# Which engine makes the low halves of the first expert product's panels: a one-argument change in a Trainium2 kernel

## The chip, the cores and the metric

The kernel runs on one core of one Trainium2 chip. A core has five engines with queues of their own: TensorE (PE: matmuls, and PEld: weight loads beside them), VectorE (DVE), ScalarE (ACT), GpSimd (POOL) and SyncE (SP, which here only issues DMAs). Each engine works its own queue in order; engines meet through semaphores. The metric is the device time of one execution, in microseconds (us).

## The reference, cut to what matters

The model is a chain of two blocks over 512 tokens of width 1024: a gated delta rule layer and a sliding-window attention layer, then a layer that mixes an mLSTM with forgetting attention, and at its end a product-key retrieval over 16384 experts of one neuron each. Only this last part is touched by the change:

```python
def block(xb):                       # 128 tokens
    scores = einsum('thpc,hpnc->thpn', (xb @ w_query)..., keys32)
    val, idx = lax.top_k(scores, 16)              # per head and half
    top_s, pos = lax.top_k(cand, 16)              # of 16 x 16 sums
    ids = ...                                     # 8 heads x 16 experts per token
    gate = softmax(top_s)
    act = gelu(einsum('ted,td->te', u_emb[ids], xb))
    return einsum('te,ted->td', gate * act, v_emb[ids])
```

The kernel computes three of the four blocks of 128 tokens densely: gelu of all 16384 first products, times a dense gate matrix G that is zero outside the chosen experts, times all of `v`. For the fourth block (tokens 0 to 127) it gathers the chosen rows of `u` and `v`.

## The kernel before, in words

All large products are made in split float32: an operand is written as a high half (rounded to the fast matmul type by ACT, line 233) and a low half (the operand minus its high half, line 235), and three matmuls (lines 315 to 317, `mm3`) make the product. `halves` does this for a panel of 128 x 1024: the cast is always on ACT, and the subtraction is on DVE, or on POOL if the caller passes `lo_on_pool=True`. Panels of the earlier stages come from `Feed`, which passes it; so does `route1`, with the 16 panels of the query weights.

`stage_p` is the last stage, from about 1517 us of the profile on. Its parts are these.

- `route1` (line 1495 on): the queries, their scores and the first choice of 16, all tokens.
- The stretch ahead of the loop, about 1637 to 2009 us. `route2` makes the second choice of 16 for each of the four token blocks on DVE (`top16`, line 1534 and after, rows by line 1561 and after). `build_g` builds the dense gates G for three token blocks in 32 steps each: two one-hot tiles `o0` (DVE, line 1598) and `o1` (in one of four steps POOL, line 1601, four instructions; else DVE, line 1603), `o0` times the gate (in two of four steps POOL, line 1605; else ACT, line 1608), four small matmuls into `pG` (line 1611), an ACT copy, and every eight steps a DMA of the result to DRAM. Woven between these are 48 (`SPILL`) jobs of class `First`. In this stretch a planner orders the instructions of each engine's queue when the kernel is built.
- The loop, about 2009 us to the end. Its order is written out by hand (`manual_schedule`): 208 jobs, 80 `First` and 128 `Second`, of which the first six are `First`, the last ten `Second`, and between them about five `First` to eight `Second`. At step n the code issues the loads of job n, the preparations of job n-1 and the matmuls of job n-2 (`LEAD = 2`), and after the preparation the late uses of gathered rows (DVE, `LATE = 2` gathers behind their issue) and the issue of new gathers (POOL, line 1470).

A `First` loads one panel of `u` transposed (`raw`, 512 KB, line 1348), makes its halves `whi` (ACT) and `wlo` (line 1351 calls `halves`), multiplies in 24 matmuls of 384 columns into `pj`, and applies gelu on ACT into `hg` (line 1357). A `Second` loads a panel of `v` (line 1412), multiplies `hg` by the gates on DVE (`W`, line 1417), splits `W` (ACT `Wh`, line 212, and DVE `Wl`, line 213), makes the panel's halves `whio` (ACT) and `wloo` (DVE, line 235), and multiplies in 18 matmuls of 512 columns into six accumulators `acc`.

The 256 gathers (128 of rows of `u`, then 128 of `v`) are indirect DMAs issued by POOL; each is used by one DVE instruction: line 1474 (row product with `xt`, summed) or line 1479 (scaled and added to `x`). Panels of `u`, panels of `v` and gathered rows share one ring of eight `raw` buffers; the tiles `whi` and `wlo` have two buffers each.

The lines that the change and the steps below speak of: 221 to 236 (`halves`), 1351 (`First.prep`), 1353 to 1361 (`First.work`), 1414 to 1420 (`Second.prep`), the loop with `ld.load()`, `pr.prep()` and `wk.work()`, and `gather`.

Of the kernel before, what the change touches and what calls it, by code (L numbers as in the profile page):

```python
# [1327 lines left out]
def stage_p(k, out):  # L1328
# [3 lines left out]
    with pool(tc, name="sp1", bufs=1) as s1:  # L1332
# [7 lines left out]
        class First:  # L1340
# [7 lines left out]
                nc.sync.dma_start(self.raw, a["uT"][self.i])  # L1348

            def prep(self):  # L1350
                self.pan = k.halves(self.raw, lo_on_pool=True, bufs=2)

            def work(self):
                p = k.acc()
# [300 lines left out]
```

## Time and profile before

| what | us |
|---|---|
| median of three runs | 2926.01 |
| lowest and highest of them | 2915.71, 2930.39 |
| the profiled execution | 2929.05 |
| its span, first to last instruction | 2927.3 |

The page gives the busy time of each engine over the span, its course in 40 slices of 73 us, and groups of instructions. Further views of the trace are the busy time in chosen stretches, the waits of a stretch grouped by who waited for whom, the instructions grouped by line and shape, and the instructions in order of time. In a group of instructions "idle before" is the idle time of the engine just before them, and the arrow names what ended it. A DVE instruction's duration runs some 0.07 us into that of the next one, so busy times of a stretch, which count an instant once, are a little below the sum of durations.

### The profile page before, as it was taken

The page shows a single profiled execution, that of the slowest core. Times are in us where ns is not written, and L with a number is a line of the kernel's source. Part 1 is how long each engine was busy: PE and PEld are TensorE (multiplying, and loading weights), DVE is VectorE, ACT ScalarE, POOL GpSimd, SP SyncE. Part 2 cuts the span into 40 slices and gives each one's busy share as a digit, 9 for nine tenths or more (in the row PEclk, how much of TensorE's full clock was granted, in tenths as well). Part 3 has the DMA queues.
Part 4 walks back from the last instruction along what each step waited for, and adds up shares of the span by engine and source line. Part 5 has one row for each costly group of instructions (what it writes and reads, how often), then busy time and mean ns, then how long its engine had stood idle before and what let it go on. Part 6 is the DMA issues. An engine that isn't in the chain of part 4 may idle for free.

```text
span 2927.3 us, 39434 instructions
## 1 busy us (share of the span) xinstructions
PE 2759.3 (94%) x14291; PEld 2266.0 (77%) x14291; DVE 2048.9 (70%) x4211; ACT 1126.7 (38%) x2300; POOL 1112.6 (38%) x737
## 2 busy tenths in 40 slices
PE   7999999989999999899989888899999999999998
PEld 5777777767676777677668788799888888888887
DVE  6666666675565556445657999955888888888887
ACT  5444444344434334233322254554333333333332
POOL 0100000000101133331113488797666665666652
PEclk9999999999999999998799998899999999999999
DMA  4111111122122122210022333456889899888886
GB/s 145 51 58 58 58 58 58 44 79 66 58 66 65 58 66 63 72 58 30 15 94 80 106 137 132 174 184 249 307 314 322 294 319 320 299 309 306 310 307 233
DMA packets 170463, 440.92 MB, mean 151 GB/s; under 512 B 13932, under 2 KB 79756, under 8 KB 168604
## 3 DMA queue, kind: packets, MB, share of 16 engines
q1 hardware_dynamic: 133404, 304.17, 30.9%
q0 software_dynamic: 36864, 134.23, 12.5%
q8 instruction: 113, 1.85, 0.3%
q14 instruction: 82, 0.67, 0.1%
HBM read 401.60 MB, written 36.75 MB: 150 GB/s over the span
## 4 chain that ended last, share of the span: by engine, by line
PE 47%; DVE 21%; issue 13%; DMA 7%; ACT 6%; POOL 5%; ACTq 0%; SPq 0%; POOLq 0%; DVEq 0%
PE pj L315 8%; PE pj L316 8%; PE pj L317 8%; DVE x L1479 5%; DVE raw L1474 4%; ACT whio L233 3%; POOL wlo L235 2%; DMA raw<-in_uT_dram 2%; PE pG L1611 2%; DMA raw<-in_u_dram,ids 2%; DVE W L1417 2%; DVE wloo L235 1%; POOL o L1601 1%; PE po L922 1%; PE fo L1305 1%
## 5 line engine op out<-in xcount | busy, mean ns | idle before, releaser
L315 PE MATMUL pj<-hThi,whi 128*128 128x384 f32 (+2 forms) x1664 | 606.3, 365 | 4.6 <-ACT hg L1357 3.9
L317 PE MATMUL pj<-hThi,wlo 128*128 128x384 f32 (+2 forms) x1664 | 598.0, 359 | 5.0 <-POOL wlo L235 4.8
L316 PE MATMUL pj<-hTlo,whi 128*128 128x384 f32 (+2 forms) x1664 | 600.2, 361 | 0.0
L235 POOL TENSOR_TENSOR wlo<-raw,whi 128x1024 fp32r<-128x1024 f32 x144 | 368.5, 2559 | 366.8 <-ACT whi L233 339.1
L315 PEld LDWEIGHTS pj<-hThi,whi 128*128 128x128 f32 x1664 | 319.9, 192 | 32.9 <-ACT hg L1357 4.2
L317 PEld LDWEIGHTS pj<-hThi,wlo 128*128 128x128 f32 x1664 | 319.0, 192 | 31.1 <-POOL wlo L235 10.5
L316 PEld LDWEIGHTS pj<-hTlo,whi 128*128 128x128 f32 x1664 | 319.7, 192 | 24.4 <-DVE hTlo L213 0.7
L316 PE MATMUL acc<-wloo,Wh 128*128 128x512 f32 x768 | 307.8, 401 | 22.8 <-DVE wloo L235 21.0
L315 PE MATMUL acc<-whio,Wh 128*128 128x512 f32 x768 | 301.5, 393 | 0.6 <-ACT whio L233 0.4
L317 PE MATMUL acc<-whio,Wl 128*128 128x512 f32 x768 | 300.3, 391 | 0.0
L212 ACT CAST Wh<-W 128x384 fp32r<-128x384 f32 x128 | 65.7, 514 | 479.2 <-DVE W L1417 469.4
L1474 DVE SCALAR_TENSOR_TENSOR raw<-raw,xt 128x1024 f32<-128x1024 f32 x128 | 225.6, 1795 | 34.1 <-DMA raw<-in_u_dram,ids 25.6
L1479 DVE SCALAR_TENSOR_TENSOR x<-raw,act,x 128x1024 f32<-128x1024 f32 x128 | 237.7, 1857 | 3.8 <-DMA raw<-in_v_dram,ids 1.6
L233 ACT CAST whi<-raw 128x1024 fp32r<-128x1024 f32 x144 | 150.3, 1044 | 144.6 <-issue 106.5
L316 PEld LDWEIGHTS acc<-wloo,Wh 128*128 128x128 f32 x768 | 144.1, 188 | 78.5 <-DVE wloo L235 51.4
L1470 POOL DMA_INDIRECT raw<-in_u_dram,ids x128 | 186.8, 1459 | 37.1 <-issue 24.5
L235 POOL TENSOR_TENSOR wlo<-wraw,whi 128x1024 fp32r<-128x1024 f32 x52 | 124.2, 2402 | 188.0 <-ACT whi L233 187.9
L235 DVE TENSOR_TENSOR wloo<-raw,whio 128x1024 fp32r<-128x1024 f32 x128 | 156.8, 1225 | 49.8 <-ACT whio L233 49.8
L1470 POOL DMA_INDIRECT raw<-in_v_dram,ids x128 | 170.2, 1329 | 49.5 <-issue 26.3
L315 PEld LDWEIGHTS acc<-whio,Wh 128*128 128x128 f32 x768 | 144.1, 188 | 32.0 <-ACT whio L233 4.0
L317 PEld LDWEIGHTS acc<-whio,Wl 128*128 128x128 f32 x768 | 144.2, 188 | 28.4
L682 POOL TENSOR_TENSOR kbe<-qk,beg 128x512 f32<-128x512 f32 x8 | 8.4, 1051 | 378.4 <-DVE qk L575 378.4
(417 smaller groups left out, 5620.6 us busy)
## 6 DMA issues: line engine op xcount, KB each, us to landing
raw<-in_uT_dram SPq DMA_DIRECT2D x128, 512.0 KB, 4.1
raw<-in_v_dram SPq DMA_DIRECT2D x128, 512.0 KB, 6.7
wraw<-in_wa_dram SPq DMA_DIRECT2D x48, 512.0 KB, 3.6
G<-stage SPq DMA_DIRECT2D x12, 2048.0 KB, 7.2
Gt<-G SPq DMA_DIRECT2D x32, 768.0 KB, 8.4
wraw<-in_wb_dram SPq DMA_DIRECT2D x32, 512.0 KB, 3.8
wraw<-in_wmt_dram SPq DMA_DIRECT2D x20, 512.0 KB, 3.5
H<-hg SPq DMA_DIRECT2D x48, 192.0 KB, 2.5
```

What stands on the lines that cost most here:

```text
L212: self.nc.scalar.copy(hi, src)
L233: nc.scalar.copy(hi, raw)
L235: eng.tensor_tensor(out=lo, in0=raw, in1=hi.bitcast(F32), op=ALU.subtract)
L315: nc.tensor.matmul(out, wh, mh, start=first, stop=False)
L316: nc.tensor.matmul(out, wh, ml, start=False, stop=False)
L317: nc.tensor.matmul(out, wl, mh, start=False, stop=last)
L922: nc.tensor.matmul(po[:, (4 * b + h) * 64 : (4 * b + h + 1) * 64], PT[:, h * nst + st, :], V[:, s0 // P + st, g * 64 : (g + 1) * 64], star ...
L1417: nc.vector.tensor_tensor(out=split_t(w), in0=split_t(hold.pop(self.i)), in1=gates[self.i // 4][:, :, self.i % 4, :], op=ALU.mult)
L1470: nc.gpsimd.indirect_dma_start(out=g, out_offset=None, in_=src, in_offset=bass.IndirectOffsetOnAxis(ap=ids[:, j : j + 1], axis=0))
L1474: nc.vector.scalar_tensor_tensor(g, g, 1.0, xt0, op0=ALU.mult, op1=ALU.mult, accum_out=act[:, j : j + 1])
L1479: nc.vector.scalar_tensor_tensor(k.x[:, 0, :], g, act[:, j : j + 1], k.x[:, 0, :], op0=ALU.mult, op1=ALU.add)
L1611: nc.tensor.matmul(p[:, n * P : (n + 1) * P], o1[:, n, :], o0[:, n, :], start=True, stop=True)
```

## The change

`First.prep` no longer passes `lo_on_pool=True`, so that the subtraction of line 235 is issued on DVE for the 128 panels of the first product: 48 ahead of the loop and 80 in it. POOL keeps the one-hot tiles and gate products of `build_g`, the panels of `route1` and of the earlier stages, and the issue of the gathers. Buffers, loads and the order of the loop's code stay.

```diff
             def prep(self):
-                self.pan = k.halves(self.raw, lo_on_pool=True, bufs=2)
+                self.pan = k.halves(self.raw, bufs=2)
```

## Rows read from the trace of the kernel before

**Rows 1.** The page: busy us of each engine (share of the span), instructions
```profile
PE 2759.3 (94%) x14291; PEld 2266.0 (77%) x14291; DVE 2048.9 (70%) x4211; ACT 1126.7 (38%) x2300; POOL 1112.6 (38%) x737
```

**Rows 2.** Busy time by stretch: stretch, its us, engines, PE clock, DMA share, GB/s
```profile
1640.00:1900.00 260.00, 213.32 (x1241) 204.42 (x1240) 255.66 (x515) 127.21 (x266) 193.55 (x125) 0.90 0.42 145
1900.00:2009.00 109.00, 104.10 (x667) 103.12 (x667) 60.25 (x58) 59.32 (x132) 97.82 (x69) 0.96 0.45 161
2009.00:2923.00 914.00, 888.33 (x4231) 762.97 (x4229) 752.58 (x773) 303.16 (x418) 557.62 (x333) 1.00 0.87 306
```

**Rows 3.** Waits of the loop, 2009 to 2923 us: total us, times, longest
```profile
POOL wlo L235 <- ACT whi L233: 205.8, 67, 5.9
...
DVE Wl L213 <- ACT Wh L212: 85.3, 128, 1.4
PEld acc L316 <- DVE wloo L235: 51.4, 78, 1.1
...
DVE wloo L235 <- ACT whio L233: 49.8, 128, 1.0
```

**Rows 4.** Instructions by line and shape, loop: count | busy us, mean ns | idle before
```profile
L1479 DVE SCALAR_TENSOR_TENSOR x<-raw,act,x 128x1024 f32<-128x1024 f32 x128 | 237.7, 1857 | 3.8 <-DMA raw<-in_v_dram,ids 1.6
L1474 DVE SCALAR_TENSOR_TENSOR raw<-raw,xt 128x1024 f32<-128x1024 f32 x127 | 224.3, 1800 | 25.8 <-DMA raw<-in_u_dram,ids 25.6
L235 DVE TENSOR_TENSOR wloo<-raw,whio 128x1024 fp32r<-128x1024 f32 x128 | 156.8, 1225 | 49.8 <-ACT whio L233 49.8
...
L235 POOL TENSOR_TENSOR wlo<-raw,whi 128x1024 fp32r<-128x1024 f32 x79 | 202.9, 2568 | 233.2 <-ACT whi L233 205.8 <-PE acc L317 27.4
```

**Rows 5.** Single lines, whole span: duration ns min/median/max, first and last start
```profile
L1474 DVE SCALAR_TENSOR_TENSOR raw<-raw,xt x128: 1212/1220/3546, 1965.5 to 2451.7; 128x1024 f32<-128x1024 f32 x128
L1479 DVE SCALAR_TENSOR_TENSOR x<-raw,act,x x128: 1276/1285/3427, 2453.6 to 2918.1; 128x1024 f32<-128x1024 f32 x128
L1598 DVE TENSOR_TENSOR o<-cst,selT x96: 664/692/2887, 1688.0 to 1998.9; 128x512 f32<-128x512 f32 x96
...
L1534 DVE TENSOR_TENSOR cand<-val x32: 398/418/2617, 1643.8 to 1856.2; 128x256 f32<-128x256 f32 x32
```

**Rows 6.** In order of time, loop: start us, duration us, engine, line, instruction
```profile
2203.47 1.04 ACT L233 CAST whi<-raw 128x1024 fp32r<-128x1024 f32 x1
...
2204.59 2.48 POOL L235 TENSOR_TENSOR wlo<-raw,whi 128x1024 fp32r<-128x1024 f32 x1 [2.25 <-ACT whi L233]
2204.74 3.41 DVE L1474 SCALAR_TENSOR_TENSOR raw<-raw,xt 128x1024 f32<-128x1024 f32 x1
...
2208.08 1.22 DVE L1474 SCALAR_TENSOR_TENSOR raw<-raw,xt 128x1024 f32<-128x1024 f32 x1
```

**Rows 7.** The same view, TensorE: first of the loop, three starts of jobs, last
```profile
2009.47 0.42 PE L315 MATMUL pj<-hThi,whi 128*128 128x384 f32 x1
...
2208.86 0.34 PE L315 MATMUL pj<-hThi,whi 128*128 128x384 f32 x1
...
2213.06 0.39 PE L315 MATMUL acc<-whio,Wh 128*128 128x512 f32 x1
...
2221.37 0.34 PE L315 MATMUL pj<-hThi,whi 128*128 128x384 f32 x1
...
2922.07 0.39 PE L317 MATMUL acc<-whio,Wl 128*128 128x512 f32 x1
```

**Rows 8.** Instructions by line and shape, ahead of the loop: 1637 to 2009 us
```profile
L1598 DVE TENSOR_TENSOR o<-cst,selT 128x512 f32<-128x512 f32 x96 | 95.5, 1001 | 37.8 <-PE pG L1611 23.6 <-ACT selT L1577 10.7 <-POOL wlo L235 3.4
L1603 DVE TENSOR_TENSOR o<-cst,selT 128x512 f32<-128x512 f32 x72 | 68.8, 956 | 0.0
L1534 DVE TENSOR_TENSOR cand<-val 128x256 f32<-128x256 f32 x32 | 28.0, 885 | 0.0
...
L235 POOL TENSOR_TENSOR wlo<-raw,whi 128x1024 fp32r<-128x1024 f32 x48 | 125.3, 2611 | 48.3 <-ACT whi L233 48.0
```

**Rows 9.** The same view and stretch, TensorE: matmuls that waited for POOL
```profile
L1611 PE MATMUL pG<-o,o 128*128 128x128 f32 x764 | 110.6, 296 | 40.2 <-POOL o L1605 21.9 <-POOL o L1601 7.6 <-ACT o L1608 4.5
```

## The prediction

> **What bounds the kernel now.** The page comes first: TensorE is busy for 94% of the span, DVE for 70%, POOL for 38% [rows 1]. That is an average over stages, and it would call TensorE the bound and DVE free. The next view is therefore the busy time by stretch [rows 2]. Only two stretches hold instructions that the change moves. In the one ahead of the loop DVE is busy for 255.7 of the first 260 us and TensorE for only 213; from 1900 us on it is TensorE for 104 of 109 us, and DVE for 60. The change's cost is to be read there from DVE in the first part and from TensorE in the second.
>
> The loop takes 914 us. TensorE is busy for 888 of them and DVE for 753. The third view, the waits of the loop, shows that DVE's 161 idle us are not free: 85.3 and 49.8 us of them are waits inside a `Second`'s own chain, DVE for ACT's `Wh` and DVE for ACT's `whio`, 128 times each [rows 3]. DVE can't use them, since its queue goes in order and the next instruction in it needs what ACT is making. Another 25.6 us are waits for gathers [rows 4], nearly all at the loop's start. 752.6 + 85.3 + 49.8 + 25.6 = 913.3 us: **DVE's queue is full for the whole loop**. And TensorE waits for it: its weight loads for `wloo` sat 51.4 us, in 78 of 128 jobs [rows 3].
>
> TensorE's own need comes from the starts of undisturbed jobs. A `First` goes from 2208.86 to 2213.06, 4.20 us; two `Second` follow from there to 2221.37, 4.15 us each [rows 7]. 80 x 4.20 + 128 x 4.15 = 867 us. The loop's matmuls run from 2009.47 to 2922.07, 913 us with the last one. So 46 us of the loop are TensorE standing still, and DVE's queue sets the loop, with TensorE close behind.
>
> **Why DVE is so full.** The groups of the loop show lines 1474 and 1479 at a mean of 1.800 and 1.857 us [rows 4], but their medians are 1.220 and 1.285 us and their longest 3.5 and 3.4 us [rows 5]. In order of time the reason shows: line 1474 starts at 2204.74, just after POOL's `wlo` has begun (2204.59 for 2.48 us), and takes 3.41 us; the same instruction, started at 2208.08 with no POOL subtraction beside it, takes 1.22 [rows 6]. 3.41 is about what is left of POOL's 2.48 and a whole 1.22 behind it. So a DVE instruction with two operands stands still while POOL's subtraction runs. In the loop the excess is 127 x (1.800 - 1.220) + 128 x (1.857 - 1.285) = 73.7 + 73.2 = **147 us of DVE's time**, and apart from `wlo` POOL does nothing there but issue gathers.
>
> **The loop, after.** DVE takes on 80 subtractions. The nearest row is its own `wloo`, the same shape, 1.225 us [rows 4]: +98 us. It loses the stretch: -147 us. DVE's queue then needs 753 + 98 - 147 = 704 us of work; with the waits of the chain, 135 us, 839 us, and with the start's wait for gathers, some of which the new subtractions fill, 865 at most. TensorE needs 867. The bound passes to TensorE. I don't take the floor. Per `Second` DVE has about 0.55 + 0.57 + 1.23 of work, 1.05 of chain waits and 1.27 gathers (256 over 202 steps) of 1.25, 5.0 us against TensorE's 4.15; per `First` 1.23 + 1.6 = 2.8 against 4.20. Pairs of `Second`, and the last ten jobs, which are all `Second`, still run DVE late by a microsecond or two before a `First` gives it back. For this I leave 8 us, about a sixth of the 46. Loop: 913 to 875, **-38 us**. Bounds: the floor, -46, and below it nothing; on the other side two thirds of TensorE's stalls stay, -15.
>
> The new wait is DVE's for `whi`, and behind it in DVE's queue stand the uses of gathers and the next `W` and `wloo`. `whi` is 1.04 us of ACT. In the shown place it starts at 2203.47 and is done at 2204.5, before DVE goes from `wloo` to the gathers at 2204.74 [rows 6]. Laying the written order of the jobs over the trace, `whi` is finished when DVE would come to it for 67 of the 80 panels, and for all but four of the rest it is late by under 0.15 us or in the loop's first steps, where DVE waits for gathers anyway. I cost it at nothing there; without that cover it is the second rival. POOL's queue loses 203 us and its waits for `whi`, 205.8 us, in front of gathers [rows 3, 4], so gathers go out earlier; the ring of eight `raw` buffers and the uses on DVE, not POOL, then hold them back. The loop moves its data 4% faster, a DMA share of about 0.91 for 0.87 [rows 2]. That isn't full, and I cost it at nothing. SP's loads wait for the same ring, and `wlo`'s end on DVE releases a panel's buffer at about the time that POOL's did.
>
> **Ahead of the loop.** DVE takes on 48 x 1.225 = 58.8 us. It loses stretch here too: line 1598 96 x (1.001 - 0.692) = 29.7, line 1603, of the same shape, 72 x (0.956 - 0.692) = 19.0, line 1534 32 x (0.885 - 0.418) = 14.9, together 63.6 us [rows 5, 8]. But POOL has other work here that can hold DVE up, and `wlo` is 125.3 of its 291.4 busy us, 43% [rows 2, 8]. By that share 27 us go, at best all 64. DVE's work changes by -5 to +32 us. Where that falls before 1900 us it is paid in full, since DVE is the bound; behind it DVE has 49 us idle. Against it, TensorE's waits for POOL's `o` tiles, 21.9 + 7.6 us [rows 9], shrink with a POOL queue 43% shorter. POOL waits 48.0 us for `whi` here [rows 8]; how much of that DVE takes over depends on where the planner puts the subtraction, between nothing and all. The ends are -30 us (the waits of TensorE gone, DVE even) and +48 (all the waits of `whi`, or DVE's +32 and some of them). I take +5, nearest to the rows on DVE's work, with a third of it hidden behind 1900 us and some of TensorE's waits gone.
>
> **Sum.** -38 + 5 = -33 us on the profiled 2929.05: 2896. The median of the runs lies 3 us below the profiled execution, so the forecast is **2893 us**, 1.1% less.
>
> **Rivals.** (1) *The stretch ahead of the loop eats the gain.* DVE is full there for 260 us, and if the planner puts subtractions in front of gate tiles that TensorE waits for, it grows by 20 to 48, say 34: 2926 - 38 + 34 = 2922. For it speaks DVE's 255.7 of 260; against it the 49 idle us behind.
> (2) *DVE stands at the head of its queue for `whi`* in the loop, as POOL did for 205.8 us. ACT's `whi` stands behind a `gelu` that waits for TensorE; if DVE comes early, it waits about a `gelu` and a cast. Up to 28 us of such waits are hidden (867 - 839), and 46 more only undo the gain, so this decides from 74 us on, 0.9 us for each panel. At POOL's full 206 us the loop would be 867 + 178 = 1045, and the whole 2926 + 132 + 5 = 3063; at 1.7 us a panel, 136 us, the loop is 975 and the kernel 2926 + 62 + 5 = 2993. The 67 of 80 speak against it.
> (3) *The stretch of DVE's instructions isn't POOL's subtraction's doing* (but, say, the gathers'). Then nothing is given back: 888 + 98 = 986 for the loop, +73, and +39 ahead: 3038. The pair in [rows 6] speaks against it. The Trainium skill, "Perfetto Trace Analysis", section "Optimizing Scalar/DVE Operations", says that with DVE saturated, moving some of its work to ScalarE or even GpSimd may make sense, which is the reverse of this change; by that rule taken alone this rival's time would come. The same section adds that the two share a read port, so that moving between them might not help, and that is what [rows 6] show.
> (4) *Ahead of the loop it pays as well*: with TensorE's waits for POOL gone, -25 there: 2926 - 38 - 25 = 2863.
>
> The change does what it says, as the default of `halves` is DVE; that it leaves the subtraction on POOL is no case.
>
> **How the numbers follow.** Forecast 0.66, (1) 0.17, (2) 0.05, (3) 0.03, (4) 0.09. Measurements of this kernel tell about 0.5% from no change, 14.6 us. The forecast with its bounds in the loop alone reaches from 2885 to 2916; the range takes in (4) and most of (1): 2862 to 2932. Faster by over 0.5% is under 2911.4: nearly all of the forecast and (4), and little of (1), 0.75. Within 0.5%: the rest of the forecast and most of (1), 0.14. Slower by over 0.5%: (2), (3) and the far end of (1), 0.11.
>
> **What would show it.** Right: lines 1474 and 1479 at means near 1.22 and 1.29 in the loop; DVE's busy time in it near 700 us, though 80 subtractions came; the waits of weight loads for `wloo` far below 51 us; the loop's matmuls within 10 or 15 us of 867; waits of DVE for `whi` of a few us. Wrong: those two lines stay stretched (3); DVE waits for `whi` by tens of us (2); the loop's first matmul starts later than 2030 us (1). The step that I trust least is the stretch ahead of the loop, whose queues the planner orders anew.

## The result, and the profile after

The changed kernel takes 2850.53 us (median of six runs, 2843.90 to 2858.38) where the kernel before takes 2928.20 (six runs, 2915.71 to 2935.66). The ratio is 0.9733, with a 95% interval of 0.9712 to 0.9754: 2.7% less. Forecast were 2893 us and 1.1%, and a range from 2862 to 2932; the direction is right, the time lies below the range, and the forecast size is less than half of what came.

The profiled execution took 2848.16 us, 80.9 less than that of before. The starts of TensorE's matmuls divide it into three parts: up to the first matmul of a `First`, from there to the last `pG` (the stretch ahead of the loop), and the loop. Busy time by stretch, first of the kernel before, then of the changed one; the columns are those of [rows 2]:

```profile
1635.58:2009.47 373.89, 322.31 (x1939) 312.25 (x1937) 318.94 (x588) 188.53 (x400) 293.75 (x194) 0.92 0.42 149
2009.47:2922.07 912.60, 887.48 (x4227) 762.50 (x4225) 751.65 (x772) 302.69 (x418) 557.62 (x333) 1.00 0.87 306
```

```profile
1626.15:1962.42 336.27, 306.06 (x1938) 300.98 (x1937) 309.53 (x634) 188.41 (x400) 205.32 (x149) 0.95 0.50 172
1962.42:2841.51 879.09, 872.55 (x4227) 766.24 (x4225) 686.65 (x853) 302.05 (x418) 371.44 (x251) 1.00 0.90 315
```

| part | before | after | difference | forecast |
|---|---|---|---|---|
| up to the first `First` | 1635.6 | 1626.2 | -9.4 | 0 |
| ahead of the loop | 373.9 | 336.3 | -37.6 | +5 |
| loop | 912.6 | 879.1 | -33.5 | -38 |

The loop came nearly as forecast. The whole miss is ahead of it, but for 9 us in a part whose code is the same; kernels below that don't touch that part start their first `First` between 1622 and 1636 us, so it says nothing of the change.

In the loop, the instructions by line answer to [rows 4]:

```profile
L1479 DVE SCALAR_TENSOR_TENSOR x<-raw,act,x 128x1024 f32<-128x1024 f32 x128 | 163.8, 1280 | 1.0
...
L1474 DVE SCALAR_TENSOR_TENSOR raw<-raw,xt 128x1024 f32<-128x1024 f32 x128 | 154.0, 1219 | 0.0
L235 DVE TENSOR_TENSOR wlo<-raw,whi 128x1024 fp32r<-128x1024 f32 x79 | 96.6, 1222 | 54.9 <-ACT whi L233 54.8
```

The excess over the medians is gone to the last: 1.857 and 1.800 us have become 1.280 and 1.219, and the new subtraction costs 1.222. DVE's busy time fell from 752 to 687 us although 80 instructions came. The waits of the loop answer to [rows 3]:

```profile
ACT hg L1357 <- PE pj L317: 189.5, 79, 3.8
DVE Wl L213 <- ACT Wh L212: 86.2, 128, 1.4
...
DVE wlo L235 <- ACT whi L233: 54.8, 35, 4.8
DVE wloo L235 <- ACT whio L233: 53.7, 128, 1.6
...
PEld acc L316 <- DVE wloo L235: 18.5, 34, 1.1
```

TensorE's weight loads now wait 18.5 us for `wloo`, not 51.4. DVE waits 54.8 us for `whi`, in 35 of 80 panels, which the forecast put at a few us. It is the reverse side of the gain: DVE is ahead, and ACT's `whi` stands in ACT's queue behind a `gelu` that waits for TensorE (in order of time, that holds for 49 of the 54.8 us). TensorE itself waits for `wlo` nowhere in the loop. 686.7 + 86.2 + 54.8 + 53.7 = 881 us, the loop's 879 to within 2, so DVE's queue is full again, but some 50 us of it are now waits that end when TensorE is ready.

Ahead of the loop the instructions by line of DVE, POOL and TensorE answer to [rows 8, 9]:

```profile
L1598 DVE TENSOR_TENSOR o<-cst,selT 128x512 f32<-128x512 f32 x96 | 77.6, 815 | 5.0 <-PE pG L1611 5.0
L235 DVE TENSOR_TENSOR wlo<-raw,whi 128x1024 fp32r<-128x1024 f32 x48 | 63.9, 1331 | 16.8 <-ACT whi L233 16.8
L1603 DVE TENSOR_TENSOR o<-cst,selT 128x512 f32<-128x512 f32 x72 | 52.3, 727 | 0.0
...
L1601 POOL TENSOR_SCALAR o<-cst,selT 128x128 f32<-128x128 f32 x96 | 111.1, 1169 | 68.0 <-ACT selT L1577 63.2 <-PE pG L1611 4.6
L1605 POOL TENSOR_TENSOR o<-o,selT 128x512 f32<-128x512 f32 x48 | 89.1, 1858 | 62.5 <-DVE o L1598 62.4
...
L1611 PE MATMUL pG<-o,o 128*128 128x128 f32 x764 | 100.8, 284 | 17.3 <-POOL o L1605 11.6 <-POOL o L1601 5.6
```

DVE took on 63.9 us of subtractions here, and its busy time fell from 318.9 to 309.5: 73 us of its other instructions' time went. POOL's gate products (line 1605) grew, from a mean of 1.432 us in the trace of before to 1.858, where they now stand behind DVE; POOL has the time for it. TensorE's idle time fell from 373.9 - 322.3 = 51.6 us to 336.3 - 306.1 = 30.2: its waits at the gate products (line 1611) went from 40.2 us [rows 9] to 17.3, its waits for low halves from 3.3 to 10.9. Its busy time, for the same matmuls, fell by 16.2 us, with the granted clock at 0.95 for 0.92.

The stretch ahead has a part in which DVE is full and a tail in which TensorE is. The last instruction of `route2` on DVE (line 1571) marks the border; both parts, before and after:

```profile
1635.58:1889.50 253.92, 210.41 (x1226) 202.01 (x1225) 248.91 (x520) 120.26 (x248) 187.37 (x120) 0.90 0.39 136
1889.50:2009.47 119.97, 111.90 (x714) 110.24 (x714) 70.02 (x69) 68.27 (x152) 106.38 (x74) 0.96 0.49 176
```

```profile
1626.15:1896.45 270.30, 240.24 (x1498) 235.71 (x1497) 263.35 (x584) 147.13 (x309) 161.64 (x111) 0.94 0.47 161
1896.45:1962.42 65.97, 65.82 (x442) 65.28 (x441) 46.18 (x51) 41.29 (x92) 43.69 (x39) 1.00 0.63 218
```

DVE's part grew by 16 us, and the tail shrank by 54: TensorE has 442 matmuls left in it, where it had 714. In DVE's queue 129 of the 168 one-hot tiles (lines 1598 and 1603) now stand ahead of line 1571, where there were 101, so more of TensorE's work is ready while DVE is still full.

### The profile page after: what moved, and what is told of

Read it like the earlier page. It is cut to its first block, busy times and chain, and to the rows that moved or that the text cites. A ratio compares the mean times of both kernels' runs of the same rounds, so it can differ in the third digit from the quotient of the medians.

```text
span 2846.4 us, 39369 instructions
## 1 busy us (share of the span) xinstructions
PE 2718.2 (95%) x14291; PEld 2250.7 (79%) x14291; DVE 1973.7 (69%) x4339; ACT 1126.0 (40%) x2300; POOL 836.2 (29%) x609
## 4 chain that ended last, share of the span: by engine, by line
PE 66%; DVE 16%; issue 7%; ACT 5%; DMA 3%; POOL 3%; SPq 0%; ACTq 0%; DVEq 0%; POOLq 0%
PE pj L315 11%; PE pj L316 11%; PE pj L317 10%; PE acc L316 4%; PE acc L317 4%; PE acc L315 3%; PE pG L1611 2%; ACT whio L233 2%; DVE x L1479 2%; DMA raw<-in_v_dram 2%; PE po L922 1%; DVE wloo L235 1%; PE fo L1305 1%; PE po L316 1%; PE po L315 1%
## 5 line engine op out<-in xcount | busy, mean ns | idle before, releaser
L317 PE MATMUL pj<-hThi,wlo 128*128 128x384 f32 (+2 forms) x1664 | 593.5, 357 | 10.9 <-DVE wlo L235 10.9
L1470 POOL DMA_INDIRECT raw<-in_v_dram,ids x128 | 191.7, 1498 | 238.1 <-DVE wloo L235 120.9
L235 DVE TENSOR_TENSOR wlo<-raw,whi 128x1024 fp32r<-128x1024 f32 x128 | 161.7, 1263 | 71.7 <-ACT whi L233 71.6
L235 DVE TENSOR_TENSOR wloo<-raw,whio 128x1024 fp32r<-128x1024 f32 x128 | 156.9, 1226 | 53.7 <-ACT whio L233 53.7
L316 PEld LDWEIGHTS acc<-wloo,Wh 128*128 128x128 f32 x768 | 144.2, 188 | 46.1 <-DVE wloo L235 18.5
L1479 DVE SCALAR_TENSOR_TENSOR x<-raw,act,x 128x1024 f32<-128x1024 f32 x128 | 163.8, 1280 | 1.0
L1474 DVE SCALAR_TENSOR_TENSOR raw<-raw,xt 128x1024 f32<-128x1024 f32 x128 | 154.0, 1219 | 0.0
L233 ACT CAST whi<-wraw 128x1024 fp32r<-128x1024 f32 x100 | 104.4, 1047 | 107.0 <-PE pj L316 68.3
```

Of the source, the lines that this page charges most:

```text
L233: nc.scalar.copy(hi, raw)
L235: eng.tensor_tensor(out=lo, in0=raw, in1=hi.bitcast(F32), op=ALU.subtract)
L316: nc.tensor.matmul(out, wh, ml, start=False, stop=False)
L317: nc.tensor.matmul(out, wl, mh, start=False, stop=last)
L1470: nc.gpsimd.indirect_dma_start(out=g, out_offset=None, in_=src, in_offset=bass.IndirectOffsetOnAxis(ap=ids[:, j : j + 1], axis=0))
L1474: nc.vector.scalar_tensor_tensor(g, g, 1.0, xt0, op0=ALU.mult, op1=ALU.mult, accum_out=act[:, j : j + 1])
```

## The experiments

**Do the two parts add up?** Two kernels make the change on one side of the loop's start alone.

```diff
-                self.pan = k.halves(self.raw, lo_on_pool=True, bufs=2)
+                self.pan = k.halves(self.raw, lo_on_pool=self.i >= SPILL, bufs=2)   # e1_ahead
+                self.pan = k.halves(self.raw, lo_on_pool=self.i < SPILL, bufs=2)    # e2_loop
```

> Only the 48 panels ahead of the loop have their low halves made by DVE; the 80 of the loop stay on POOL. The trace of the changed kernel puts 38 us of its gain ahead of the loop and 34 in the loop, and some 9 ahead of both, where nothing changed. If the two parts add up, this kernel's stretch ahead of the loop is about 336 us for 374, its loop about 913 us as before, and its time some 38 us below the kernel before: about 2890. If the loop's gain rested on what the stretch ahead leaves behind (gathers issued earlier, DVE free at the loop's start), the loop is shorter too, 895 or less.

> Only the 80 panels of the loop have their low halves made by DVE; the 48 ahead stay on POOL. If the parts add up: stretch ahead 374 us as before, loop about 879, time some 34 us below the kernel before: about 2894. If the predicted floor of TensorE in the loop (867 us) is right, the loop can't be below that in any case.

Measured: ahead alone 2893.7 us (ratio to before 0.989, 0.9846 to 0.9934), loop alone 2886.5 (0.9873, 0.9826 to 0.9921), beside 2928.8 for the kernel before. 35.1 + 42.4 = 77.5 us, and both together gave 77.7; the intervals are some 13 us wide to either side, so that it fits so closely is chance. By stretch, first ahead alone, then loop alone (stretch ahead, loop):

```profile
1621.56:1957.12 335.56, 303.88 (x1938) 298.27 (x1937) 309.63 (x635) 188.56 (x400) 206.65 (x147) 0.96 0.47 165
1957.12:2869.38 912.26, 887.08 (x4227) 762.91 (x4225) 750.36 (x772) 302.55 (x418) 557.26 (x333) 1.00 0.88 306
```

```profile
1626.90:1998.37 371.47, 322.14 (x1939) 311.82 (x1937) 319.63 (x587) 188.98 (x400) 293.81 (x196) 0.92 0.45 156
1998.37:2876.19 877.82, 871.70 (x4227) 766.27 (x4225) 686.45 (x853) 302.10 (x418) 370.83 (x251) 1.00 0.90 315
```

Each part shortens its own stretch, to 335.6 and 877.8 us, and leaves the other where it was. The loop's gain doesn't rest on what the stretch ahead leaves behind. The two can be explained apart.

**Is it POOL's reading that holds DVE up, or POOL's being busy?** Two kernels put work without use back on POOL in the changed kernel, one that reads and one that only writes.

```diff
                 self.pan = k.halves(self.raw, bufs=2)
# d1_read, DUM = 928
+                nc.gpsimd.tensor_tensor(out=dum, in0=xt0[:, 0:DUM], in1=xt0[:, 0:DUM], op=ALU.subtract)
# d2_write, dum of 720 columns
+                for _ in range(3):
+                    nc.gpsimd.memset(dum, 0.0)
```

> The changed kernel, and for each of the 128 panels POOL gets a subtraction of 928 columns whose result nobody reads and whose operands are long there (about 2.2 us each by the 2.4 us of 1024 columns). Theory A, a POOL subtraction holds up DVE's instructions with two operands: the stretch comes back on lines 1474, 1479, 1598 and 1603, DVE has its own 128 subtractions besides, the loop becomes 879 plus some 85 us (147 us of stretch times 928/1024, less the 30 us that DVE had spare and 15 that it needn't stretch), the stretch ahead of the loop 20 to 50 us longer: about 2960. Theory B, POOL's queue is what delayed the gate tiles ahead of the loop, and DVE's stretch is incidental: stretch ahead back at 374, loop as in the changed kernel, 2888. Theory C, the planner's new order alone brought the gain ahead of the loop: near 2850.

> The changed kernel, and for each of the 128 panels POOL gets three memsets of 720 columns, which only write and read nothing (about 0.73 us each by the 0.53 us of a memset of 528 columns in the trace of before, so 2.2 us for a panel, as much of POOL's time as in the run with the subtraction). Theory A with the hold-up coming from reads: nothing changes, lines 1474 and 1479 stay at 1.22 and 1.28 us, 2850. Theory A with any POOL work holding DVE up: as the run with the subtraction, about 2960. Theory B, POOL's queue: stretch ahead of the loop back at 374 us without stretch on DVE, 2888.

Measured: 2957.6 us with the reads (1.0117, 1.0071 to 1.0163), 2872.8 with the writes (0.9824, 0.9781 to 0.9867). The number of the first run is the expected one, and not for the reason given. In both kernels the useless work waits for nothing, so the planner put the part of the 48 panels ahead of the loop almost wholly further forward, into the queries; with the reads the first `First` starts at 1681 us, 55 later than in the changed kernel. The stretch ahead, 340.5 and 336.3 us, thus had none of the reads and a fraction of the writes, and says nothing. The loop, whose order is written out, does. In it, with the reads:

```profile
2021.70:2950.28 928.58, 886.48 (x4226) 765.87 (x4225) 792.00 (x853) 300.82 (x418) 521.18 (x327) 1.00 0.86 298
...
L213 DVE TENSOR_TENSOR Wl<-W,Wh 128x384 fp32r<-128x384 f32 x128 | 139.4, 1089 | 88.4 <-ACT Wh L212 87.8 <-issue 0.7
...
L1420 DVE TENSOR_TENSOR W<-hg,Gt 128x384 f32<-128x384 f32 x80 | 70.3, 879 | 0.0
...
L1354 POOL TENSOR_TENSOR dum<-xt 128x928 f32<-128x928 f32 x76 | 139.2, 1831 | 1.5
```

and with the writes:

```profile
1976.20:2852.34 876.14, 871.14 (x4226) 768.63 (x4225) 686.62 (x853) 302.21 (x418) 529.71 (x479) 1.00 0.90 316
...
L213 DVE TENSOR_TENSOR Wl<-W,Wh 128x384 fp32r<-128x384 f32 x128 | 71.5, 558 | 86.2 <-ACT Wh L212 85.5 <-issue 0.7
...
L1355 POOL MEMSET dum<- 128x720 f32 x228 | 161.0, 706 | 8.8
```

POOL is as busy in the loop in both, 521 and 530 us. With the reads DVE's work goes from 687 to 792 us and the loop from 879 to 929; with the writes both stay (876). As a whole the run with writes is 22 us longer than the changed kernel, where 0 were expected; in its trace the first `First` starts 14 us later, and neither the stretch ahead nor the loop is longer. The hold-up now falls on other lines than before, `Wl` (1.089 us for 0.558) and `W` (0.879 for 0.552), since the useless subtraction waits for nothing and so starts at another point of DVE's round (at 2308.10 us, for one, right behind the issue of a gather; `Wl`, started at 2308.38, took 1.89 us). The Trainium skill, "SBUF — State Buffer", section "Who interferes with whom", says that a DVE instruction with two inputs in SBUF contends with a GpSimd instruction that reads SBUF and not with one that only writes it, and that the later one stands still until the first is done; the 0.558 us beside memsets and the 1.089 beside subtractions agree with it. The loop grew by 50 us where 85 were expected: with the hold-up back, DVE's waits for ACT's casts (`Wh`, `whio`, `whi`) went from 195 us to 138, so part of the hold-up lies in what had been waits.

**What makes the stretch ahead of the loop 37.6 us shorter?** Three kernels change only what POOL and DVE do for the 48 panels; the loop is that of the kernel before. The instructions of TensorE, DVE and ACT, but for the subtractions, stand in the same order, one by one, as in the kernel before.

```diff
-                self.pan = k.halves(self.raw, lo_on_pool=True, bufs=2)      # for i < SPILL:
+                nc.gpsimd.tensor_tensor(out=lo, in0=xt0, in1=xt0, op=ALU.subtract)        # e6_read
+                for _ in range(3): nc.gpsimd.memset(lo[:, 0:768].bitcast(F32), 0.0)       # e4_write
+                nc.gpsimd.memset(lo[:, 768:1024].bitcast(F32), 0.0)
+                self.pan = hi, hold["lo"]                                                 # e3_none
```

> As the run in which POOL writes zeros ahead of the loop, but POOL makes each low half by one subtraction of a long finished tile from itself (zeros too, about 2.4 us): it reads, needn't wait for the panel, and the low halves are left out of the 48 products. The order of the instructions of TensorE, DVE and ACT is the same, one by one, in this kernel, in the one that writes and in the kernel before, so the planner's order is out of the comparison. Theory A (POOL's reads hold DVE up, and DVE POOL): the stretch ahead of the loop goes from the 324 us of the writing run back to 355 to 375, lines 1598 and 1603 back to 0.95 to 1.00 us: near 2915. Theory B (POOL's queue, whose length is 115 us of these against 119 of memsets): 324, lines 1598 and 1603 at 0.79 and 0.70, near 2875.

> The kernel before, but ahead of the loop POOL writes zeros into each low half (four memsets, some 2.6 us a panel by 0.53 us for 528 columns) in place of the subtraction, which leaves the low halves out of these 48 products. POOL's queue is as long as before and the memsets stand in the same place of the code; they read nothing, and DVE takes on nothing. Theory A (hold-up of DVE by POOL's reads): as the run without low halves ahead of the loop, so about 302 to 336 for 374. Theory B (POOL's queue delays gate tiles): about 374, or some 20 us less. Theory C (planner's order): no number of its own, but DVE's lines 1598 and 1603 would stay at their 1.00 and 0.96 us.

> The kernel before, but ahead of the loop only the first panel's low half is made (on DVE); the other 47 panels use it as theirs, so that neither engine makes theirs, which leaves out 47 subtractions and changes the products. The loop stays as before. It is the end of the scale for the 374 us of the stretch ahead of the loop: with DVE's own 59 us the stretch took 336. Theory A (POOL's subtraction held DVE up and cost far more of DVE's time than the 59 us that it takes there): 336 or less, down to TensorE's floor of about 302 (48 x 4.2 us, and some 100 us of small matmuls). If DVE's added 59 us cost their full length: 336 - 59 = 277, below that floor, so 302 to 310. If DVE's added work is hidden: about 330.

Measured: 2906.0, 2880.5 and 2866.1 us (0.9927, 0.9837 and 0.9791 of before; intervals 0.9899 to 0.9955, 0.9789 to 0.9884, 0.9746 to 0.9836). The stretch ahead and line 1598 (1607 or 1606 in these kernels), with reads, with writes, with none:

```profile
1627.06:1978.98 351.92, 316.18 (x1938) 309.94 (x1937) 302.32 (x588) 189.39 (x400) 276.71 (x194) 0.93 0.48 158
...
L1607 DVE TENSOR_TENSOR o<-cst,selT 128x512 f32<-128x512 f32 x96 | 100.2, 1051 | 38.2 <-PE pG L1620 25.6 <-ACT selT L1586 11.1 <-POOL o L1610 1.6
```

```profile
1635.26:1959.43 324.17, 305.82 (x1939) 301.77 (x1937) 251.34 (x588) 189.54 (x400) 275.33 (x335) 0.95 0.51 171
...
L1607 DVE TENSOR_TENSOR o<-cst,selT 128x512 f32<-128x512 f32 x96 | 75.5, 793 | 57.2 <-PE pG L1620 43.0 <-ACT selT L1586 7.0 <-POOL wlo L1358 3.9
```

```profile
1632.53:1946.46 313.93, 298.04 (x1938) 294.75 (x1937) 251.91 (x588) 189.22 (x400) 174.62 (x147) 0.98 0.52 177
...
L1606 DVE TENSOR_TENSOR o<-cst,selT 128x512 f32<-128x512 f32 x96 | 77.4, 812 | 48.4 <-PE pG L1619 40.6 <-ACT selT L1585 5.4 <-POOL o L1609 2.3
```

This is a scale with steps. From the kernel before to reads that wait for nothing and are a little shorter (2.09 us for 2.61): 373.9 to 351.9, -22. From reads to writes at the same length of POOL's queue (276.7 and 275.3 us busy): -28, and DVE's busy time from 302 to 251. From writes to nothing: -10. From there to the changed kernel, where DVE makes the low halves: 336.3, +22. -22 - 28 - 10 + 22 = -38. So theory A (POOL's reads hold DVE up) holds for the largest single step, theory B (POOL's queue is too long) for the 10 us, each read from one profiled execution of a kernel; theory C (the planner's order) is out for the first three steps, whose order is the same. Along the scale TensorE's waits at the gate products fell too, from 40.2 us before to 30.9, 15.5 and 14.2. Reading didn't bring the whole 374 back: the expected 355 was missed by 3 us. Whether the first 22 come from the shorter subtraction or from POOL's waits for `whi` (48 us, [rows 8]) is not separated.

The last step, +22, is a sum of two. The two parts of the run with none are

```profile
1632.53:1839.20 206.67, 190.78 (x1211) 187.49 (x1210) 199.50 (x520) 120.47 (x248) 114.39 (x89) 0.98 0.51 168
1839.20:1946.46 107.26, 107.26 (x730) 107.26 (x729) 52.41 (x70) 68.75 (x152) 60.23 (x58) 1.00 0.54 193
```

From there to the changed kernel DVE's part grows by 64 us, from 207 to 270, with 38 of the subtractions and 28 more one-hot tiles in it, and TensorE's tail shrinks by 41, from 107 to 66. So DVE pays for its subtractions here, and the planner's new order gives much of it back by having less left for the tail. Theory C is thus not out for this step; no run has the new order without the change, so what the order is worth alone stays open.

**Do smaller pieces do as well?** If a DVE instruction stands behind what is left of one POOL instruction, pieces should hold it up less, and nothing need be moved. The edit, shortened:

```diff
-        eng.tensor_tensor(out=lo, in0=raw, in1=hi.bitcast(F32), op=ALU.subtract)
+        for i in range(4):                                  # 256 columns each, on POOL
+            cs = slice(i * 256, (i + 1) * 256)
+            eng.tensor_tensor(out=lo[:, cs], in0=raw[:, cs], in1=hi[:, cs].bitcast(F32), op=ALU.subtract)
```

> The kernel before with every low half of the 128 panels made on POOL in four pieces of 256 columns (0.6 us each, if the 2.4 us divide). Nothing is moved to another engine. Theory A: a DVE instruction waits for what is left of the piece that runs, at most 0.6 us for 2.4, and the pieces then wait for DVE in their turn; the stretch of lines 1474 and 1479 falls from 147 us to 40 to 80, the loop from 913 to about 880 to 890, and the stretch ahead of it to 345 to 360: 2870 to 2885. If DVE is held up by all of a panel's pieces in a row, or for another reason: 2929, stretch as before.

Measured: 2960.6 us, 1.0133 of before (1.0096 to 1.0170), so 1.3% longer, where 2870 to 2885 were expected. The two stretches, the pieces in the loop, and one place in order of time (POOL, then DVE):

```profile
1635.97:2008.09 372.12, 321.61 (x1939) 310.72 (x1937) 296.41 (x588) 189.39 (x400) 337.82 (x338) 0.91 0.44 149
2008.09:2953.79 945.70, 898.05 (x4227) 769.48 (x4225) 686.52 (x772) 305.88 (x418) 667.26 (x570) 0.99 0.82 296
...
L238 POOL TENSOR_TENSOR wlo<-raw,whi 128x256 fp32r<-128x256 f32 x316 | 357.8, 1162 | 150.4 <-ACT whi L233 122.5 <-PE acc L320 24.8 <-PE acc L319 1.8
...
2310.96 5.87 POOL L238 TENSOR_TENSOR wlo<-raw,whi 128x256 fp32r<-128x256 f32 x4 [2.24 <-ACT whi L233]
...
2311.11 1.76 DVE L1477 SCALAR_TENSOR_TENSOR raw<-raw,xt 128x1024 f32<-128x1024 f32 x1
...
DVE raw L1477 <- DMA raw<-in_u_dram,ids: 61.1, 17, 11.6
```

DVE's part of the theory came true: its instructions stand 0.54 us behind a piece (1.76 for 1.22), and its busy time fell to 296 and 687 us, lower than in the changed kernel ahead of the loop and the same in it. But the two engines now take turns, piece by piece, and POOL needs 5.87 us for this panel; over the loop it is 4 x 1.162 = 4.65 us in the mean, where it was 2.57 [rows 4]. The pieces alone would cost some of that, as the shortest took 0.72 us, 2.87 for four. Behind the pieces in POOL's queue stand the gathers in the loop and the gate tiles ahead of it: in the loop DVE's waits for gathers rose from 27 to 84 us (lines 1477 and 1482), and its waits for the loads of `hs` and `Gt` from 3 to 41; the stretch ahead stayed at 372. What makes those loads late was not followed. **A shorter DVE didn't help while POOL paid for it.**

**Versions that go further.** If the hold-up is the price, then no subtraction that DVE could make belongs on POOL, and ahead of the loop no gate tile either.

```diff
# all four, on top of the change
-            self.pans.append(self.k.halves(self.raw[i], bufs=self.bufs, gain=self.srcs[i][1], lo_on_pool=True))
+            self.pans.append(self.k.halves(self.raw[i], bufs=self.bufs, gain=self.srcs[i][1], lo_on_pool=False))
-        pan = k.halves(r, lo_on_pool=True, bufs=2)
+        pan = k.halves(r, bufs=2)
# g1_o1 and g3_both: o1
-        if b % 4 == 0:
+        if False:
# g2_gate and g3_both: o0 times the gate
-        if b % 4 in (1, 3):
+        if False:
```

> The changed kernel with the low halves of all panels on DVE, also those of the 16 query panels and of the 52 panels of the stages before, which POOL made (some 160 us of POOL's time). DVE is busy for about 60% of those stages, and in the trace of the changed kernel the excess of its instructions beside these subtractions sums to 42 us. Theory A: DVE takes on 68 x 1.22 = 83 us and loses 42 us, in stretches where TensorE is busy for 94% and DVE isn't the bound: 0 to 20 us less, about 2840. If TensorE waits for DVE's chains there: 10 to 30 us more.

> The kernel with all low halves on DVE (2808), and the one-hot tiles of line 1601 on DVE too, as the other three of four are (24 x 0.69 = 17 us for DVE, 111 us less for POOL). If what is left of hold-ups ahead of the loop (lines 1598, 1603 and the subtractions run some 20 us over their shortest) and TensorE's 17 us of waits for POOL's tiles go: 335 to 320, about 2795. If DVE's 17 us are paid in full, as it is the bound until 1900 us: 335 to 345, about 2815.

> The kernel with all low halves on DVE, and the gate product of line 1605 on ACT in all steps, as it is in two of four (48 x 4 x 0.395 = 76 us for ACT, which is busy for 188 of 335 us; 89 us less for POOL). TensorE's waits for this tile (11.6 us) go, and its hold on DVE: 335 to 320, about 2795. If ACT's casts of panels then come late behind the 76 us: 335 or more, 2808 to 2830.

> Both of the last two: ahead of the loop POOL has nothing but the issue of gathers, so no hold-up of DVE is left; lines 1598 and 1603 at 0.68 us. DVE +17 us less some 20 of stretch, ACT +76. If the shared hold-up is what is left: about 315 for 335, 2788. If DVE's and ACT's own lengths bound it: 335 to 345, 2808 to 2818.

Measured: all low halves on DVE 2807.7 us (0.9608, 0.9574 to 0.9641), 43 less than the changed kernel, where 0 to 20 were expected; with `o1` on DVE 2809.9 (0.9587, 0.9558 to 0.9616), with the gate product on ACT 2799.4 (0.9558, 0.9529 to 0.9586), with both 2796.9 (0.9544, 0.9509 to 0.9578). The stretch ahead in these four, in this order:

```profile
1604.88:1940.24 335.36, 303.39 (x1939) 298.20 (x1937) 309.49 (x634) 188.34 (x400) 204.48 (x149) 0.96 0.50 172
```

```profile
1590.94:1927.33 336.39, 302.88 (x1938) 298.38 (x1937) 317.31 (x658) 189.66 (x400) 109.78 (x53) 0.96 0.50 172
```

```profile
1588.74:1914.71 325.97, 302.95 (x1938) 297.33 (x1937) 282.65 (x634) 246.99 (x592) 139.25 (x101) 0.96 0.51 177
```

```profile
1594.09:1909.21 315.12, 298.59 (x1939) 295.45 (x1937) 293.11 (x658) 244.84 (x592) 5.94 (x5) 0.97 0.53 184
```

The first gains in the stages before: its first `First` starts at 1604.9 us, 21 before that of the changed kernel, as TensorE's idle time up to there falls from 86.9 to 63.0 us, and its stretch ahead is the same. This trace, of 2824.9 us, is the longest of its five runs, so it shows 21 of the 43 us only. `o1` alone is a wash: what POOL no longer holds up, DVE pays itself. The gate product on ACT takes 10 us off, and with both, the stretch is 315 us, with POOL idle. These intervals overlap for the last three, but each run with `o1` alone (2807.8 to 2812.5) is longer than each of the other two kernels (up to 2803.3); between those two the order is open. All four lie below the changed kernel's 0.9712 to 0.9754.

## Why the prediction was right in the loop and wrong ahead of it

- *DVE's queue sets the loop, and POOL's subtraction is why it is full.* Right. The excess of lines 1474 and 1479 went whole, 147 us, and the loop alone gave 34 to 35 us of the 38 forecast. Putting a reader back on POOL brought 105 us of DVE's time back, a writer none.
- *The bound passes to TensorE, at 867 and 8 us.* Right: 879. By the starts of its jobs TensorE has 12 us of stalls left, 10 in runs of two `Second` and 2 in the last ten jobs, the two places that the prediction names.
- *The wait for `whi` costs nothing.* Right in its price, wrong in its size: 54.8 us of waits in 35 panels, where a few us in 13 were forecast. 28 us were said to be hidden and 74 the point of decision; what was not seen is that a DVE ahead of TensorE must wait there, and that such waits are no loss.
- *Rivals.* (3), that the excess has another cause, is refuted by the pair of runs with reads and writes. (2) showed as waits without loss. (1) was on the wrong side. (4) has the direction that came, but its -25 was too little and its way only in part the one that showed: of TensorE's 29.5 us of waits for POOL's tiles 12 went and 17.3 stayed.
- *Ahead of the loop, +5.* This is the step that failed: -37.6 us came, by a term mis-sized and by terms left out. Mis-sized: DVE's relief was taken at 27 us by POOL's share of busy time (43%), with 64 as the best case; DVE got back 73, 47 of them at the three lines that the 64 counted. A share of busy time was the wrong key. Laid over each other in the trace of before, DVE's instructions run about 93 us over the usual time of their shape in this stretch: 64 of these beside the subtraction, 25 beside line 1605 and 4 beside line 1601. Left out for the most part: TensorE, which stands behind both. The sum treated DVE as the bound until 1900 us, asked how long its queue would be, and set against it only some of TensorE's waits for POOL's tiles. Its busy time did fall only by 9 us; but TensorE's idle time fell by 21, mostly at the gate products, and TensorE's own 322 busy us became 306 at a granted clock of 0.95 for 0.92. These 16 us had no term at all: TensorE's busy time was taken as fixed. The same goes along the three runs: 316, 306 and 298 us busy at 0.93, 0.95 and 0.98, with 36, 18 and 16 us idle; that the clock rises because the gaps close is likely, but not shown. Left out as well: the tail. The prediction says that the planner orders these queues anew and trusts the step least for it, but has no term for work of TensorE that comes to stand beside DVE's full part; that took 54 us off the tail while DVE's part grew by 16.
- *The range.* Its lower end was rival (4), -38 in the loop and -25 ahead. The loop kept within that; the stretch ahead went beyond it and beyond its own bound of -30, which counted TensorE's waits for POOL's tiles (29.5 us) as all there was to win.

## What to carry to other kernels

Before a subtraction with two operands is given to POOL to relieve DVE, look at the mean and the median of DVE's own instructions beside it: here 80 subtractions of 1.22 us each were kept off DVE at a price of 147 us of its time. Where two engines hold each other up, the shorter queue of one is not the gain; read what the third engine waits for, and how much of its work is left when the fuller engine is done; its granted clock can change too. Cutting the holder into pieces moves the wait to its own queue, so look at what stands there before cutting.

## What the runs showed of the hardware that was not expected

- The hold-up changes hands at each instruction: with four pieces for one, POOL took 4.65 us in the mean for the 1024 columns of a panel in the loop where it took 2.57, and DVE's instruction beside them took 1.76 us for 1.22 in the place shown.
- POOL's subtraction of 928 columns from a tile by itself took 1.74 us at the median, and of 1024 columns 2.09 us in the mean, both less by the column than a panel's subtraction from two different tiles, 2.34 us at its shortest.
- POOL's memsets held up no DVE instruction with two f32 operands: 228 of them in the loop, 161 us, and DVE's instructions at their shortest. They did hold up DVE's small casts. In the run that writes zeros ahead of the loop, line 1565 (`af`, 0.20 us at its shortest) starts just behind a memset of 0.74 us at 1836.10 and takes 0.76; its median over eight is 0.64 us, where line 1556, the same cast, has 0.21 in the kernel before (that run first):

```profile
L1565 DVE CAST af<-au x8: 201/640/822, 1661.7 to 1836.2; 128x128 bf16<-128x128 uint32 x8
...
L1556 DVE CAST af<-au x8: 203/214/1070, 1667.3 to 1876.1; 128x128 bf16<-128x128 uint32 x8
```

- The issue of gathers, 251 in the loop of the changed kernel each about 1.5 us of POOL's time, didn't hold DVE up either: line 1474 at 1.219 us in the mean.
